# A two-layer decoder trunk on one core: stores, adds and row loads of the first layer's last head re-placed, and two small matmul groups of the second layer re-formed

## The chip, the cores and the metric

The kernel runs on one core of one Trainium2 chip. The metric is device microseconds of one execution; less is better. The core's engines are named as in the profile: PE (TensorE), DVE (VectorE), ACT (ScalarE), POOL (GpSimd), SP (SyncE); PEld is the loading of weights into PE.

## The reference, cut to what matters

Two residual layers over x of 512 tokens by 2048 channels, everything in fp32.

```python
for i in range(2):
    hn = rms_norm(x, norm_w[i])
    x = x + (diff_attention_mixer if i == 0 else rwkv7_mixer)(hn, ...)

# layer 0: 8 heads, two sets of scores each, 256 value channels per head
q, k, v, gate = split(h @ w_in)                      # w_in 2048 x 8192
q, k = rope(rms_norm(q)), rope(rms_norm(k))
a = softmax(q0 k0) - lam * softmax(q1 k1)            # causal
o = rms_norm(a @ v) * (1 - lambda_init) * silu(gate)
out = o @ w_out

# layer 1: RWKV-7, 32 heads of 64 channels
r, k, v, g, dw, da = split(mix(h @ w_in))            # mix: with the token before
kk = k * k_k
kk = kk / max(sqrt(sum over a head's channels of kk * kk), 1e-12)
for t in range(512):                                 # S: 64 x 64 per head
    S = S * w[t] + (S @ -kk[t]) (kk * a)[t]^T + v[t] k[t]^T
    y[t] = S @ r[t]
out = (group_norm(y) + bonus) * silu(g) @ w_out
```

## The kernel before, in words

Matrix products that need fp32 accuracy are made of three products of halves: each operand is a high part (wh, hH) and the rest (wl, hL), and `mm3` sums high x high, high x low, low x high. ACT casts wh from the loaded tile wraw (L105), DVE subtracts to get wl (L106). The 512-column matmuls named pp at L122 and L568 are most of PE's work.

**First layer.** The heads come one after the other. `unit_head` makes the projections of head h by products of blocks in halves of the matrix (a 2 x 2 scheme with fewer products), group by group: `all_groups` goes over N = 4 weight tiles, for each the split (L105, L106), then 12 matmuls at L568. Ta, Tb, Tc, Td (`g.Ts`, name `chained`) are four weight tiles of 512 KB that stay and are turned from one block's weights into the next by an accumulating DMA that POOL issues (`add_w`, L86), which adds another block of the matrix in memory to the tile. For the last head (h = 7, `last`) the order is: y, the block of T, S1, S2, `square`, `third`, S4. During S2 each of Ta to Td gets its next addend after its products, and four more tiles b0 to b3 (`b22`, named wraw) get theirs, for `third`. `s4` loads ("reloads") four more weight tiles on SP's queue into wraw.

While head h's matmuls run, the attention of head h - 1 is carried out in steps: a `Chain` counts matmuls (`tick`) and puts a step behind every so many of them. For one block of 128 tokens the steps are scores, softmax, turned weights (L364), weighted values o, norm, then `turn_y`: the 128 x 256 outputs y are transposed into PSUM (yt), ACT writes their high part yTh (L399), DVE the rest yTl (L401), and ACT issues the stores of both to the scratch tensors ys (L386). yTh has a place of its own, yTl one with the tag "th", one buffer each. Tile places are named by tags; S1's sums have the places sA and sA2, S2's sB, and so on. The reciprocal square roots on DVE (rs_i, rs_t, L64 to L71) belong to the norms.

After head 7 the kernel goes on to the output projection (`unit_tok` with da_w_out, L122). Its left operand are the rows of ys, loaded back by SP into tiles hH and hL (L931), 14 pairs of 256 KB tiles; the last two pairs are head 7's and stay on the chip.

**Second layer.** The heads are taken in 16 pairs. For each pair: projections (pp at L122), decays and keys (`stage1`), `stage2`, `gram` (gp at L1304: products of all chunks of 64 tokens), a forward substitution on DVE (`t_solve`, 31 steps, L1361 and L1363), `t_combine` (below), and a scan of eight chunks (sm at L1475, L1486, L1493; ACT copies rhs at L1478 and VS at L1488 between them), then the outputs Y (L1515, L1519). They are pipelined: gp of pair j + 1 comes right after the first part of `t_combine` of pair j.

`t_combine` completes the inverse of a 64 x 64 triangular matrix from two solved halves of 32 x 32: for each head and chunk a product px <- T, G (L1394), a copy to X (L1397), and a product px <- TT, X (L1404), copied to TT (L1407). Each is a matmul of 32 rows by 32 columns, placed by `tile_position` on a 32 x 32 tile of the array: the first product has head 0 on rows 0 and columns 32, head 1 on rows 64 and columns 96. There are 8 chunks x 2 heads = 16 matmuls at each line; in the trace a plain fp32 matmul is two records, so 32. Both heads write the same PSUM tile px.

The squares of the keys are summed for each head by two matmuls at L1210 and L1211 with a matrix of ones, after a split of the squares into sHx (ACT) and sLx (DVE); the 2 x 512 result is copied (ssl, L1291) and stored by SP for `t_solve`.

The order on each engine is set when the program is built: a scheduler takes instructions by priority (`high_priority`, the offsets SOLVE and SCAN) and by the explicit `issue_after`.

Of the kernel before, what the change touches and what calls it, by code (L numbers as in the profile page):

```python
# [326 lines left out]
def attention(g, h, qkT, qkL, sq, V, VL, G, gap, rows=None, keys=()):  # L327
# [56 lines left out]

    def store(i, ts, y):
        nc.scalar.dma_start(out=g.ys[i][h * 256 : (h + 1) * 256, ts].rearrange("(c p) t -> p c t", p=P),  # L386
                            in_=y[:].bitcast(F32))

    def turn_y(t):
        pt = g.ps.tile([P, 512], F32, name="yt", tag="pb")  # L390
        for i in range(2):
            nc.tensor.transpose(pt[:, i * P : (i + 1) * P], blocks[t].y[:, i * P : (i + 1) * P], g.ident[:])
        ts = slice(t * P, (t + 1) * P)
        pv = pt[:, :256].rearrange("p (c q) -> p c q", c=2)
        if rows is None:
            hi = w.tile([P, 2, P], F32R, name="yTh", tag="yTh", bufs=1)
            lo = w.tile([P, 2, P], F32R, name="yTl", tag="th", bufs=1)
            for c in range(2):
                nc.scalar.activation(hi[:, c], pv[:, c], AF.Copy, scale=g.subw[:, c : c + 1])  # L399
            for c in range(2):  # L400
                nc.vector.scalar_tensor_tensor(lo[:, c], pv[:, c], g.subw[:, c : c + 1], hi[:, c].bitcast(F32),  # L401
                                               ALU.mult, ALU.subtract)
            store(0, ts, hi)
            due.append((1, ts, lo))
            if h == NH - 2:
                store(*due.pop())
            return
        if t == 0:
            last.extend([[g.hp.tile([P, T], F32R, name=n, tag=n) for n in ("hH", "hL")] for _ in range(2)])
        for c, (hh, hl) in enumerate(last):  # L410
            nc.scalar.activation(hh[:, ts], pv[:, c], AF.Copy, scale=g.subw[:, c : c + 1])
            g.rowsplit = nc.vector.scalar_tensor_tensor(hl[:, ts], pv[:, c], g.subw[:, c : c + 1],
                                                        hh[:, ts].bitcast(F32), ALU.mult, ALU.subtract).ins
# [118 lines left out]
def unit_head(g, aps, h, t1s, sq, turned):  # L532


    nc = g.nc
    c1, c2 = qk_cols(aps, h), vg_cols(aps, h)
    acc1 = g.work.tile([P, 2, 512], F32, name="acc1", tag="acc1", bufs=1)
    acc = [None, None, acc1[:, 0], acc1[:, 1]]
    q = [t[:] for t in t1s]
    N = NH4 // KG  # L540
    last = h == NH - 1

    def pair():
        return [g.pp.tile([P, 512], F32, name="pp", tag="pp") for _ in range(2)]

    def load(i, k0, parts):
        pool, tag, bufs = (g.work, "Te", 1) if i == N - 1 else (g.wraw, "wraw", 3)
        raw = pool.tile([P, KG, 512], F32, name="wraw", tag=tag, bufs=bufs)
        load_w(g, raw, parts, k0 + i * KG, slice(0, KG))
        return raw  # L550

    def split(raw):
        return split_w(g, None, KG, 512, 0, raw)

    def block(k0, t0):
        return lambda k, t: [x[k0 + k][:, t0 + t * P : t0 + (t + 1) * P] for x in (g.hH, g.hL)]

    def form(nm, i):
        return lambda k, t: [x[:, t * P : (t + 1) * P] for x in g.sums[nm][i * KG + k]]

    def products(out, lhs, raw, start=False, end=False):
        wt = split(raw)
        for t in range(2):
            first = start
            for lo in range(2):
                for k in range(KG):
                    for x in lhs(k, t)[: 2 - lo]:
                        m = nc.tensor.matmul(out[t][:], x, wt[lo][:, k, :], start=first, stop=end and lo == 1 and k == KG - 1,  # L568
                                             skip_group_check=True)
                        tick(g, m)  # L570
                        first = False

    def all_groups(out, lhs, raw, start=False, end=False, then=None, also=None):
        added = None
        for i in range(N):
            r = raw(i)
            products(out, lhs(i), r, start and i == 0, end and i == N - 1)
            for x, k0 in [(r, then)] + ([(also[i], (c2, 0))] if also else []) if then else []:
                with g.tc.issue_after(added) if added else ExitStack():
                    added = add_w(g, x, k0[0], k0[1] + i * KG)  # L580

    def s4(out, keep, start=False, end=False):
        def raw(i):
            keep.append(load(i, NH4, c2))
            return keep[-1]
        all_groups(out, lambda i: form("S4", i), raw, start, end, None if last else (c2, 0))

    chained = lambda i: g.Ts[i]
    y = pair()
    all_groups(y, lambda i: block(NH4 + i * KG, 0), lambda i: load(i, NH4, c1), True, True)  # L590
    copy_out(g, q[:2], y)
    y = pair()
    all_groups(y, lambda i: block(i * KG, 0), chained, True, False, (c2, 0))
    take(g, q[:2], y)
    X = pair()
    all_groups(X, lambda i: form("S1", i), chained, True, last, (c2, NH4))
    copy_out(g, acc[2:], X)
    b22 = []
    if last:
        b22 += [load(i, NH4, c2) for i in range(N)]  # L600
    else:
        s4(X, b22, end=True)
        G, acc[:2] = gates(g)
        copy_out(g, acc[:2], X)
    all_groups(y, lambda i: form("S2", i), chained, then=(c1, NH4), also=last and b22)
    if last:
        G, acc[:2] = gates(g)
    take(g, acc[:2], y, ALU.subtract, acc[2:] if last else None)

    def square():  # L610
        X = pair()
        all_groups(X, lambda i: block(NH4 + i * KG, 256), chained, True, True)
        return X

    def third():
        for i in range(N):
            products(y, form("S3", i), b22[i], end=i == N - 1)
        take(g, acc[2:], y, ALU.subtract)

    head_qk(g, t1s, sq, [0, 1])  # L620
    if last:
        copy_out(g, q[2:], square())
        third()
        take(g, q[2:], y)
        head_qk(g, t1s, sq, [2, 3])
        turned()
        X = pair()
        s4(X, [], True, True)
        take(g, acc[:2], X)
        return head_vg(g, h, acc, G)  # L630
    turned()
    third()
    copy_out(g, q[2:], y)
    values = head_vg(g, h, acc, G)
    X = square()
    first_tiles(g, aps, h + 1)
    take(g, q[2:], X)
    head_qk(g, t1s, sq, [2, 3])
    return values
# [156 lines left out]
def layer0(g, aps):  # L796
# [3 lines left out]
    with ExitStack() as cx:  # L800
# [127 lines left out]
        for k in range(KT - 2):  # L928
            rows.append([g.hp.tile([P, T], F32R, name=n, tag=n) for n in ("hH", "hL")])
            for x, d in zip(rows[k], g.ys):  # L930
                loaded = nc.sync.dma_start(out=x[:].bitcast(F32), in_=d[k * P : (k + 1) * P, :]).ins  # L931
        ch = Chain(g, attention(g, h, *before, 20, rows, rest), 16)

        def all_rows(n, _):
# [279 lines left out]
def stage1(g, j, k, up):  # L1214
# [45 lines left out]

    def keys():
        nc.vector.tensor_mul(p.BK[:], p.BK[:], l[:, :, None, :].to_broadcast([P, NC_, 2, C]))
        k2 = w.tile([P, T], F32, name="k2", tag="thg", bufs=1)
        nc.scalar.activation(k2[:], k[:], AF.Square, scale=col("kk"))
        p.k2 = split_act(g, k2[:], w, "x")
        nc.vector.tensor_add(p.gam[:, 0 : NC_ - 1], m[:, 0 : NC_ - 1], m[:, 1:NC_])
        nc.scalar.activation(p.gam[:, 0 : NC_ - 1], p.gam[:, 0 : NC_ - 1], AF.Exp)

# [15 lines left out]
def gram(g, j, p, before):  # L1284

    nc, w, BK = g.nc, g.work, p.BK
    ps = g.ps.tile([P, 512], F32, name="pt", tag="pa", bufs=1)
    sum_channels(g, ps[:2, :], g.ones[:, 0 : P : C], p.k2)
    ss = w.tile([2, T], F32, name="ssl", tag="thg", bufs=1)
    with g.tc.high_priority(offset=SOLVE):  # L1290
        nc.scalar.copy(ss[:], ps[:2, :])  # L1291
        for half in range(2):
            nc.sync.dma_start(
                out=g.ltd[j % 2, half, :, :, HALF, :],
                in_=ss[:].rearrange("h (c b t) -> h c b t", c=NC_, b=2)[:, :, half, :])
    p.G = w.tile([P, NC_, 2, 2, C], F32, name="G1", tag="G1", bufs=2)
    p.BKT = w.tile([P, NC_, P], F32, name="BKT", tag="BKT", bufs=2)
    halves = []
# [73 lines left out]
def t_combine(g, j, p, lead):  # L1372
# [16 lines left out]
    yield GAP_T  # L1389
    N = NC_ * HALF  # L1390
    blocks = [(h, h * C, slice(h * C, h * C + HALF), slice(h * C + HALF, h * C + C)) for h in range(2)]
    for h, b0, lo, hi in blocks:
        for c in range(NC_):
            nc.tensor.matmul(px[hi, c * HALF : (c + 1) * HALF], p.G[lo, c, 0, h, HALF:C], T1[lo, c, :],  # L1394
                             start=True, stop=True, tile_position=(b0, b0 + HALF))
    for _, _, _, hi in blocks:
# [2 lines left out]
        r_ = slice(b0, b0 + C)  # L1399
        nc.scalar.copy(p.G[r_, :, 0, h, :], p.AR[r_, :, 0, :])  # L1400
    yield GAP_X
    for h, b0, lo, hi in blocks:
        for c in range(NC_):
            nc.tensor.matmul(px[lo, N + c * HALF : N + (c + 1) * HALF], X[hi, c, :], TT[hi, c, h, HALF:C],  # L1404
                             start=True, stop=True, tile_position=(b0 + HALF, b0))
    for h, b0, lo, _ in blocks:
# [365 lines left out]
```

## Time and profile before

| | |
|---|---|
| Time, three runs | 2114.43, 2110.9, 2113.84 us; median 2113.84 |
| Profiled execution | 2111.84 us, span 2110.1, mean granted clock 0.997 |
| PE busy | 2076.8 us, 98% of the span |
| DVE / ACT / POOL busy | 76% / 55% / 18% |
| First layer's stretch of this change | about 660 to 735 us of the span |
| Second layer's pairs | L1394 first at 1025.4, last at 1923.9 us |

A row of a timeline gives the start in us, the length in us, engine, line, operation, out<-in with shapes, the count of instructions drawn together, and in brackets the idle time of the engine before it with what ended that. A row of the windows gives the busy time and count of each engine, the granted clock of PE, the share of the DMA engines and GB/s. A row of DMA issues ends with the median us from issue to landing.

### The profile page before, as it was taken

What the parts mean: (1) busy time and instruction counts of PE and PEld (TensorE: products, weight loads), DVE (VectorE), ACT (ScalarE), POOL (GpSimd) and SP (SyncE); (2) the same over time, 40 slices, a digit from 0 to 9 for tenths busy, and PEclk for the clock granted to TensorE, in tenths of its full rate; (3) what the DMA queues carried; (4) which work ended last, traced back from release to release, by engine and by line L of the source; (5) the groups of instructions that cost most, each with busy time, mean ns of one, the idle gap of its engine ahead of it and who ended that gap; (6) DMA issues with size and microseconds to landing.
All of it is one profiled execution on the core that took longest, in us unless ns stands there. A gap on an engine that the chain in (4) does not pass through costs nothing.

```text
span 2110.1 us, 34038 instructions
## 1 busy us (share of the span) xinstructions
PE 2076.8 (98%) x11852; PEld 1690.5 (80%) x11852; DVE 1602.6 (76%) x4129; ACT 1153.6 (55%) x2278; POOL 370.4 (18%) x727
## 2 busy tenths in 40 slices
PE   9999999999999999999999999999999999999999
PEld 7888888888887788878777778888877787877887
DVE  6988888889887876576777778877777887767645
ACT  5765656566565544355465555565555556555322
POOL 1021111201112000101122221222222122221001
PEclk9999999999999999999999999999999999999999
DMA  8487877878778946623232332323333232345655
GB/s 268 153 173 190 181 170 187 166 188 177 173 183 176 307 149 179 150 88 96 90 87 89 90 90 84 94 83 92 99 95 86 85 94 86 97 138 180 190 159 121
DMA packets 159484, 294.60 MB, mean 140 GB/s; under 512 B 64352, under 2 KB 81760, under 8 KB 159312
## 3 DMA queue, kind: packets, MB, share of 16 engines
q1 hardware_dynamic: 110848, 184.91, 28.1%
q0 software_dynamic: 23808, 83.54, 21.5%
q10 hardware_dynamic: 24656, 23.97, 3.5%
q8 instruction: 93, 1.52, 0.3%
q14 instruction: 79, 0.65, 0.1%
HBM read 268.71 MB, written 23.66 MB: 139 GB/s over the span
## 4 chain that ended last, share of the span: by engine, by line
PE 74%; DVE 17%; issue 3%; ACT 3%; DMA 2%; ACTq 0%; DVEq 0%; SPq 0%
PE pp L122 33%; PE pp L568 22%; PE pt L122 4%; DVE wl L106 4%; DVE tmpl L1361 3%; DVE Tm L1363 2%; DVE VS L1497 2%; PE gp L1304 1%; ACT wh L105 1%; PE sc L122 1%; PE o L122 1%; PE sm L1475 1%; PE lora L122 1%; PE z L122 1%; PE sm L1486 1%
## 5 line engine op out<-in xcount | busy, mean ns | idle before, releaser
L106 DVE TENSOR_TENSOR wl<-wraw,wh 128x1024 fp32r<-128x1024 f32 (+2 forms) x291 | 357.7, 1229 | 211.0 <-ACT wh L105 202.2
L105 ACT CAST wh<-wraw 128x1024 fp32r<-128x1024 f32 (+2 forms) x291 | 303.6, 1043 | 266.1 <-PE pp L122 135.2
L122 PE MATMUL pp<-hL,wh 128*128 128x512 f32 x1024 | 414.7, 405 | 0.0
L122 PE MATMUL pp<-hH,wh 128*128 128x512 f32 x1024 | 413.8, 404 | 0.0
L122 PE MATMUL pp<-hH,wl 128*128 128x512 f32 x1024 | 413.6, 404 | 0.0
L122 PEld LDWEIGHTS pp<-hH,wh 128*128 128x128 f32 x1024 | 193.6, 189 | 34.3
L122 PEld LDWEIGHTS pp<-hL,wh 128*128 128x128 f32 x1024 | 193.5, 189 | 33.3
L122 PEld LDWEIGHTS pp<-hH,wl 128*128 128x128 f32 x1024 | 193.6, 189 | 32.4
L568 PE MATMUL pp<-wh,hH 128*128 128x512 f32 x448 | 176.8, 395 | 0.0
L568 PE MATMUL pp<-wh,hL 128*128 128x512 f32 x448 | 175.8, 392 | 0.0
L122 PE MATMUL pp<-wh,hH 128*128 128x512 f32 x372 | 145.6, 392 | 1.8 <-ACT hH L1092 1.8
L122 PE MATMUL pp<-wh,hL 128*128 128x512 f32 x372 | 146.4, 394 | 0.2
L122 PE MATMUL pp<-wl,hH 128*128 128x512 f32 x372 | 145.9, 392 | 0.5 <-DVE wl L106 0.5
L1481 POOL COPY SA<-VS 64x64 f32<-64x64 f32 x224 | 69.9, 312 | 425.0 <-DVE VS L1497 386.0
L1361 DVE SCALAR_TENSOR_TENSOR tmpl<-LT,Tm 128x60 f32<-128x60 f32 (+24 forms) x496 | 133.6, 269 | 11.4
L568 PE MATMUL pp<-wl,hH 128*128 128x512 f32 x448 | 140.4, 392 | 0.0
L1363 DVE TENSOR_TENSOR Tm<-Tm,tmpl 128x60 f32<-128x60 f32 (+24 forms) x496 | 104.4, 211 | 11.3
L1478 ACT COPY rhs<-sm 64x64 f32<-64x64 f32 x256 | 52.8, 206 | 89.3 <-PE sm L1475 85.9
L568 PEld LDWEIGHTS pp<-wl,hH 128*128 128x128 f32 x448 | 84.4, 188 | 17.3
L568 PEld LDWEIGHTS pp<-wh,hH 128*128 128x128 f32 x448 | 84.2, 188 | 17.3 <-issue 0.3
L568 PEld LDWEIGHTS pp<-wh,hL 128*128 128x128 f32 x448 | 84.2, 188 | 16.3
L1488 ACT COPY VS<-sm 64x64 f32<-64x64 f32 x256 | 52.7, 206 | 71.9 <-PE sm L1486 67.3
(397 smaller groups left out, 4417.6 us busy)
## 6 DMA issues: line engine op xcount, KB each, us to landing
wraw<-in_rw_w_in_dram SPq DMA_DIRECT2D x128, 512.0 KB
wraw<-in_da_w_in_dram SPq DMA_DIRECT2D x75, 512.0 KB
wraw<-in_da_w_in_dram POOLq DMA_DIRECT2D x28, 512.0 KB, 6.6
wraw<-in_da_w_out_dram SPq DMA_DIRECT2D x26, 512.0 KB
wraw<-in_rw_w_out_dram SPq DMA_DIRECT2D x26, 512.0 KB
Ta<-in_da_w_in_dram POOLq DMA_DIRECT2D x21, 512.0 KB, 5.5
Tb<-in_da_w_in_dram POOLq DMA_DIRECT2D x21, 512.0 KB, 5.5
Tc<-in_da_w_in_dram POOLq DMA_DIRECT2D x21, 512.0 KB, 5.5
```

What stands on the lines that cost most here:

```text
L105: a = nc.scalar.copy(hi[:, ks], raw[:, ks])
L106: d = nc.vector.tensor_sub(lo[:, ks], raw[:, ks], hi[:, ks].bitcast(F32))
L122: m = nc.tensor.matmul(out, a, b, start=s, stop=e, skip_group_check=skip)
L568: m = nc.tensor.matmul(out[t][:], x, wt[lo][:, k, :], start=first, stop=end and lo == 1 and k == KG - 1, skip_group_check=True)
L1304: m = nc.tensor.matmul(gp[h][:, i * P : (i + 1) * P], BK[r_, c0 + i, :, :], p.AR[r_, c0 + i, :, :], start=True, stop=True)
L1361: nc.vector.scalar_tensor_tensor(tt, LT[:, i : i + 1, i + 1 :].to_broadcast([P, s, n]), n2[:, i : i + 1], Tm[:, 0:s, i : i + 1].to_broadca ...
L1363: nc.vector.tensor_add(Tm[:, 0:s, i + 1 :], Tm[:, 0:s, i + 1 :], tt)
L1475: nc.tensor.matmul(sm[:, 0:P], both(p.G[:, c, 0]), both(VS[:, c]), start=True, stop=True)
L1478: nc.scalar.copy(rhs[r_, :], sm[r_, h * C : h * C + C])
L1481: nc.gpsimd.tensor_copy(p.SA[r_, c - 1, :], VS[r_, c, h, :])
L1488: g.copied = nc.scalar.copy(VS[r_, c, h, :], sm[r_, P : P + C])
L1497: g.state = nc.vector.scalar_tensor_tensor(VS[r_, c + 1, h, :], s_, p.gam[r_, c : c + 1], Sg[r_, :], ALU.mult, ALU.add)
```

## The change

Five edits.

1. In the attention of head 6 (`h == NH - 2`, which runs during head 7's projections) the turned outputs of all four token blocks go into one tile yT on the place sA2, each block in its own part, instead of yTh and yTl in turn.
2. In S2 of the last head the adds are issued in another order: b0 after Ta, and b1, b2, b3 after Td.
3. The loads of the rows of ys are issued behind the first reload of S4.
4. In `t_combine` both products go over chunks outside and heads inside, so that the two heads' matmuls take turns.
5. The keys' squares are kept in fp32 (no split) and summed by four matmuls of 128 tokens each, which write 32 rows apiece of one PSUM tile; the copy is 128 x 128, and the stores read it from there. k2 and ssl have places of their own.

```diff
     def store(i, ts, y):
...
-                            in_=y[:].bitcast(F32))
+                            in_=y.bitcast(F32))
...
-            hi = w.tile([P, 2, P], F32R, name="yTh", tag="yTh", bufs=1)
-            lo = w.tile([P, 2, P], F32R, name="yTl", tag="th", bufs=1)
+            if h == NH - 2:
+                if t == 0:
+                    last.append(w.tile([P, NT, 2, 2, P], F32R, name="yT", tag="sA2", bufs=1))
+                hi, lo = last[0][:, t, 0], last[0][:, t, 1]
+            else:
+                hi = w.tile([P, 2, P], F32R, name="yTh", tag="yTh", bufs=1)[:]
+                lo = w.tile([P, 2, P], F32R, name="yTl", tag="th", bufs=1)[:]
...
-            for x, k0 in [(r, then)] + ([(also[i], (c2, 0))] if also else []) if then else []:
+            adds = [(r, then, i)] if then else []
+            if also:
+                adds += [(also[n], (c2, 0), n) for n in ((0,), (), (), (1, 2, 3))[i]]
+            for x, k0, n in adds:
                 with g.tc.issue_after(added) if added else ExitStack():
-                    added = add_w(g, x, k0[0], k0[1] + i * KG)
+                    added = add_w(g, x, k0[0], k0[1] + n * KG)
...
             for x, d in zip(rows[k], g.ys):
-                loaded = nc.sync.dma_start(out=x[:].bitcast(F32), in_=d[k * P : (k + 1) * P, :]).ins
+                with tc.issue_after(g.reloaded):
+                    loaded = nc.sync.dma_start(out=x[:].bitcast(F32), in_=d[k * P : (k + 1) * P, :]).ins
...
-        k2 = w.tile([P, T], F32, name="k2", tag="thg", bufs=1)
-        nc.scalar.activation(k2[:], k[:], AF.Square, scale=col("kk"))
-        p.k2 = split_act(g, k2[:], w, "x")
+        p.k2 = w.tile([P, T], F32, name="k2", tag="k2", bufs=1)
+        nc.scalar.activation(p.k2[:], k[:], AF.Square, scale=col("kk"))
...
-    sum_channels(g, ps[:2, :], g.ones[:, 0 : P : C], p.k2)
-    ss = w.tile([2, T], F32, name="ssl", tag="thg", bufs=1)
+    for t in range(NT):
+        nc.tensor.matmul(ps[t * 32 : t * 32 + 32, :P], g.ones[:, C - 16 : C + 16].bitcast(F32),
+                         p.k2[:, t * P : (t + 1) * P], start=True, stop=True, tile_position=(0, t * 32))
+    ss = w.tile([P, P], F32, name="ssl", tag="ssl", bufs=1)
...
-    for h, b0, lo, hi in blocks:
-        for c in range(NC_):
+    for c in range(NC_):
+        for h, b0, lo, hi in blocks:
             nc.tensor.matmul(px[hi, c * HALF : (c + 1) * HALF], p.G[lo, c, 0, h, HALF:C], T1[lo, c, :],
                              start=True, stop=True, tile_position=(b0, b0 + HALF))
...
-    for h, b0, lo, hi in blocks:
-        for c in range(NC_):
+    for c in range(NC_):
+        for h, b0, lo, hi in blocks:
             nc.tensor.matmul(px[lo, N + c * HALF : N + (c + 1) * HALF], X[hi, c, :], TT[hi, c, h, HALF:C],
                              start=True, stop=True, tile_position=(b0 + HALF, b0))
```

On POOL, in S2 of the last head, the adds stood in this order before (the wraw are b0, b1, b2 and b3):

```order
L86 DMA Ta<-in_da_w_in_dram 128x1024
L86 DMA wraw<-in_da_w_in_dram 128x1024
L86 DMA Tb<-in_da_w_in_dram 128x1024
L86 DMA wraw<-in_da_w_in_dram 128x1024
L86 DMA Tc<-in_da_w_in_dram 128x1024
L86 DMA wraw<-in_da_w_in_dram 128x1024
L86 DMA Td<-in_da_w_in_dram 128x1024
L86 DMA wraw<-in_da_w_in_dram 128x1024
```

Now they stand so:

```order
L86 DMA Ta<-in_da_w_in_dram 128x1024
L86 DMA wraw<-in_da_w_in_dram 128x1024
L86 DMA Tb<-in_da_w_in_dram 128x1024
L86 DMA Tc<-in_da_w_in_dram 128x1024
L86 DMA Td<-in_da_w_in_dram 128x1024
L86 DMA wraw<-in_da_w_in_dram 128x1024 x3
```

Tc and Td moved ahead of b1, and Td ahead of b2 too. On SP, at the end of the first layer's last head, the row loads (L931) and the first reloads (wraw<-in_da_w_in) stood so before:

```order
L78 DMA T_8567<-in_da_w_out_dram 128x1024
L931 DMA hL<-ys_76 128x512
L931 DMA hH<-ys_75 128x512 x2
L931 DMA hL<-ys_76 128x512 x2
L931 DMA hH<-ys_75 128x512 x2
L931 DMA hL<-ys_76 128x512
L931 DMA hH<-ys_75 128x512
L931 DMA hL<-ys_76 128x512
L931 DMA hH<-ys_75 128x512
L78 DMA wraw<-in_da_w_in_dram 128x1024
```

and now:

```order
L78 DMA T_8560<-in_da_w_out_dram 128x1024
L78 DMA wraw<-in_da_w_in_dram 128x1024
L942 DMA hH<-ys_75 128x512
L942 DMA hL<-ys_76 128x512
L78 DMA wraw<-in_da_w_in_dram 128x1024
L942 DMA hH<-ys_75 128x512
```

The first reload moved ahead of all row loads. On ACT, at the place of `t_combine` and `gram` in one pair of the second layer, the rows were before:

```order
L1132 ACTIVATE mixr<-pp,omu 128x512
L1400 COPY G_14222<-AR 64x8x64
L1397 COPY X<-px 32x256
L1291 COPY ssl<-pt 2x512
L1397 COPY X<-px 32x256
L1400 COPY G_14222<-AR 64x8x64
L1101 COPY sHx<-mixr 128x512
L1311 COPY G_14911<-gp 128x8x64 x4
L1407 COPY TT_9520<-px 32x8x32 x2
L105 COPY wh<-wraw 128x1024
L1478 COPY rhs<-sm 64x64 x2
```

and are now:

```order
L1143 ACTIVATE mixr<-pp,omu 128x512
L1112 COPY sHx<-mixr 128x512
L1303 COPY ssl<-pt 128x128
L1409 COPY X<-px 32x256 x2
L1412 COPY G_14199<-AR 64x8x64 x2
L1323 COPY G_14886<-gp 128x8x64 x4
L1419 COPY TT_9513<-px 32x8x32 x2
L105 COPY wh<-wraw 128x1024
L1490 COPY rhs<-sm 64x64 x2
```

The cast of mixr moved ahead of the copies that follow the first px block, and ssl to the head of those copies.

More of the change, by code (lines that the diff above doesn't have):

```diff
@@ L548, in load @@
         raw = pool.tile([P, KG, 512], F32, name="wraw", tag=tag, bufs=bufs)
-        load_w(g, raw, parts, k0 + i * KG, slice(0, KG))
+        g.loaded = load_w(g, raw, parts, k0 + i * KG, slice(0, KG))
         return raw
@@ L584, in raw @@
             keep.append(load(i, NH4, c2))
+            if last and i == 0:
+                g.reloaded = g.loaded
             return keep[-1]
@@ L1287, in gram @@
     ps = g.ps.tile([P, 512], F32, name="pt", tag="pa", bufs=1)
-    sum_channels(g, ps[:2, :], g.ones[:, 0 : P : C], p.k2)
-    ss = w.tile([2, T], F32, name="ssl", tag="thg", bufs=1)
+    for t in range(NT):
+        nc.tensor.matmul(ps[t * 32 : t * 32 + 32, :P], g.ones[:, C - 16 : C + 16].bitcast(F32),
+                         p.k2[:, t * P : (t + 1) * P], start=True, stop=True, tile_position=(0, t * 32))
+    ss = w.tile([P, P], F32, name="ssl", tag="ssl", bufs=1)
     with g.tc.high_priority(offset=SOLVE):
-        nc.scalar.copy(ss[:], ps[:2, :])
-        for half in range(2):
+        nc.scalar.copy(ss[:], ps[:, :P])
+        for h in range(2):
             nc.sync.dma_start(
-                out=g.ltd[j % 2, half, :, :, HALF, :],
-                in_=ss[:].rearrange("h (c b t) -> h c b t", c=NC_, b=2)[:, :, half, :])
+                out=g.ltd[j % 2, :, h, :, HALF, :].rearrange("b (q c) t -> q c b t", q=NT),
+                in_=ss[16 * h : P : 32, :].rearrange("q (c b t) -> q c b t", c=2, b=2))
     p.G = w.tile([P, NC_, 2, 2, C], F32, name="G1", tag="G1", bufs=2)
```

## The prediction

> **What bounds the kernel now.** I read the page's busy times first, then the waits of PE, then timelines at the places that the change touches.
>
> ```profile
> PE 2076.8 (98%) x11852; PEld 1690.5 (80%) x11852; DVE 1602.6 (76%) x4129; ACT 1153.6 (55%) x2278; POOL 370.4 (18%) x727
> ```
>
> ```profile
> PE sm L1475 <- DVE VS L1497: 9.7, 28, 0.8
> PE pt L364 <- DVE rs_i L65: 5.8, 1, 5.8
> ...
> PE sm L1486 <- ACT rhs L1478: 1.5, 4, 0.4
> ```
>
> PE is busy for 98% of the span. So a change pays only where it takes matmul time off PE, or takes away one of the few waits in the second view (columns: total us, times, longest). The largest single one is 5.8 us, once, in the first layer. The profiled execution took 2111.84 us with a span of 2110.1; the median of the runs shown is 2113.84, which is 2.0 above it. I sum against the profiled execution and add the 2.0 at the end. What a measurement of this kernel can tell from no change is about 0.2%, 4.2 us.
>
> **Part 1: places of their own for head 6's outputs.** The timeline around that wait:
>
> ```profile
> 680.43 1.10 PE L568 MATMUL pp<-wh,sB 128*128 128x512 f32 x4
> ...
> 681.93 0.62 ACT L399 ACTIVATE yTh<-yt,subw 128x128 fp32r<-128x128 f32 x2 [2.36 <-DMA ys<-yTh]
> ...
> 687.08 0.35 DVE L401 SCALAR_TENSOR_TENSOR yTl<-yt,subw,yTh 128x128 fp32r<-128x128 f32 x1 [7.07 <-DMA ys<-yTl]
> ...
> 687.80 1.11 PE L364 MATMUL pt<-ident,a 128*128 128x128 f32 x4 [5.81 <-DVE rs_i L65]
> ```
>
> ```profile
> 688.57 2.05 PE L568 MATMUL pp<-wh,sB 128*128 128x512 f32 x4
> ...
> 691.27 1.54 PE L568 MATMUL pp<-wh,sB 128*128 128x512 f32 x4
> ```
>
> DVE stands 7.07 us at yTl (L401), because the one buffer of yTl is still being read by the store of the token block before. Behind it in DVE's queue are the rows of the next block's rs_i, and the transposes of PE come after those: that is the 5.81 us. After the change all four blocks have their own 2 KB in a tile on S1's second place, so neither ACT's 2.36 nor DVE's 7.07 us is left. After the idle time PE also runs slower:
>
> ```profile
> 681.00:693.00 12.00, 6.19 (x21) 4.75 (x20) 5.09 (x19) 2.31 (x5) 1.02 (x2) 0.72 1.06 213
> ```
>
> The granted clock (before the last two columns) is 0.72 in this stretch. Four matmuls at 680.43 take 1.10 us, at 688.57 they take 2.05 and at 691.27 still 1.54: 0.95 and 0.44 too much, and I put about 0.8 on the two wl matmuls between them and on the transposes. So the stall is worth 5.8 + 0.95 + 0.44 + 0.8 = 8.0 us. The new tile can be written only after S1's last matmuls have read that place; those stand a few matmuls ahead of the first turned block, so I take 0, at most 0.5 us on ACT.
>
> **Part 2: the order of the adds.** Without the stall PE comes to the next blocks 8 us earlier. The adds that make them are slow, since the DMA engines are full in that stretch (share 1.06 in the row above):
>
> ```profile
> Td<-in_da_w_in_dram POOLq DMA_DIRECT2D x1, 512.0 KB, 12.4
> ```
>
> ```profile
> 680.30 0.84 POOL L86 DMA_DIRECT2D Td<-in_da_w_in_dram  x1 [0.29 <-DVE so L378]
> ```
>
> ```profile
> 700.00 1.05 ACT L105 CAST wh<-Td 128x1024 fp32r<-128x1024 f32 x1 [0.70 <-PE pp L568]
> ```
>
> Td is issued at 680.30, lands 12.4 us later (the last number of the first row) at 692.7, and is cast at 700.00. With 8 us off, that cast comes at 692.0: in the old order it would be late by 0.7 us. In the old order Tb, b1, Tc and b2 stand before it on the queue, so the 12.4 us are up to five transfers of some 2.5 us. In the new order b1 and b2 go behind it: it lands 5 us sooner, at 687.7, 4.3 us ahead of its cast. The adds of b1 and b2 that move back are read only after all of Td's products: 0 us, at most one transfer, 2.5.
>
> **Part 3: rows behind the reload.**
>
> ```profile
> 696.80 0.33 SPq L931 DMA_DIRECT2D hL<-ys  x1
> ...
> 705.21 0.33 SPq L78 DMA_DIRECT2D wraw<-in_da_w_in_dram  x1
> ```
>
> ```profile
> 729.02 0.39 PE L122 MATMUL pp<-wh,hH 128*128 128x512 f32 x1
> ```
>
> Eleven row loads stand ahead of the first reload on SP's queue now; afterwards all 28 stand behind it. The reload waits for its buffer, which follows PE, so it moves to about 705.2 - 8 = 697.2, and the rows start then instead of at 696.8. Their first reader moves to 721, 24 us later. 0 us; if this cover were gone it would be the 8 us that the rows have not moved forward.
>
> **Part 4: second layer, two heads in turn for T, and the sums.** Each of the 16 pairs of heads has these rows (one pair):
>
> ```profile
> 1434.35 1.09 PE L1394 MATMUL px<-T,G 32*32 32x32 f32 x32
> 1435.38 0.40 PE L1210 MATMUL pt<-sHx,ones 128*2 128x512 f32 x1
> 1435.61 0.40 PE L1211 MATMUL pt<-sLx,ones 128*2 128x512 f32 x1
> 1435.94 2.06 PE L1304 MATMUL gp<-AR,BK 64*128 64x128 f32 x32
> ...
> 1442.60 0.43 PE L1486 MATMUL sm<-rhs,TT 128*128 128x64 f32 x2
> ```
>
> The px block is 32 records, 16 of one head and then 16 of the other, in 1.09 us. Do two heads overlap? Two answers of the same timeline for windows of 0.14 us, the first inside head 0, the second where head 1 begins:
>
> ```profile
> 1434.35 0.53 PE L1394 MATMUL px<-T,G 32*32 32x32 f32 x11
> ```
>
> ```profile
> 1434.56 0.50 PE L1394 MATMUL px<-T,G 32*32 32x32 f32 x14
> ```
>
> In 0.53 us 11 records run (0.03 us from one to the next, once the length of one, 0.19, is off); at the border 14 fit in 0.50: the heads do run side by side there, in the same bank. If they do so throughout, a block needs 15 steps of 0.032 and one length, 0.5 + 0.19 = 0.69 instead of 1.09, so 0.40 less. There are two such blocks for each pair (L1394, L1404): 0.80 us of PE.
>
> The sums go from two matmuls that hold PE from 1435.38 to 1435.94, 0.56 us, to four of 32 columns by 128 in plain fp32, eight records. Price per record from another row:
>
> ```profile
> 1486.52 1.20 PE L1515 MATMUL Y<-VS,G 128*64 128x64 f32 x32
> ```
>
> Here 64 moving columns in two column tiles take (1.20 - 0.2) / 31 = 0.032 us a record, as long as 32 columns on one tile above, so two column tiles run side by side. 128 columns on one tile are then 0.13: eight cost 1.0 us in a row, 0.25 four abreast. I take 0.29, nearer the row with two abreast carried on: 0.27 less. PE saves 0.80 + 0.27 = 1.07 us per pair, at most; with the sums in a row 0.36.
>
> How much of it arrives is decided by ACT, which between this block and L1486 has no gap:
>
> ```profile
> 1435.08 0.62 ACT L1400 COPY G<-AR 64x512 f32<-64x512 f32 x1 [3.15 <-PE px L1394]
> 1435.72 0.36 ACT L1397 COPY X<-px 32x256 f32<-32x256 f32 x1
> 1436.11 0.57 ACT L1291 COPY ssl<-pt 2x512 f32<-2x512 f32 x1
> ...
> 1437.73 0.62 ACT L1101 CAST sHx<-mixr 128x512 fp32r<-128x512 f32 x1
> ...
> 1442.13 0.42 ACT L1478 COPY rhs<-sm 64x64 f32<-64x64 f32 x2
> ```
>
> ```profile
> 1434.07 0.75 DVE L1280 SCALAR_TENSOR_TENSOR mixr<-mixr,prm_hrk,f 128x512 f32<-128x512 f32 x1
> ```
>
> It works from 1435.08 to the end of rhs at 1442.55, and PE starts L1486 at 1442.60, with it. In the new order the cast of mixr stands first; its input is done at 1434.82, so it fits before the chain (-0.65 with its gap), and ssl of 128 columns costs about 0.25 instead of 0.57 (-0.32; X of 256 columns costs 0.36). But ssl now leads the chain and waits for the sums, which end some 0.63 + 0.57 us after the px block's start: the chain starts at +1.2 instead of +0.73 (+0.47). Sum: -0.50 us per pair. PE would be 1.07 early and waits the other 0.57 for rhs at L1486. DVE loses one subtraction of 512 columns per pair, beside a PE that doesn't wait for it: 0. So 16 x 0.50 = 8.0 us; bounds 0 and 16 x 1.07 = 17.1 us.
>
> The Trainium skill, TensorEngine Tiling (Array Packing), Restrictions and Gotchas, says that different row tiles cannot access the same PSUM bank at the same time. Both heads of px write one bank, so by it turns would give nothing or cost; the border row above speaks against it.
>
> **The sum.** 2111.84 - 8.0 (part 1) - 0 - 0 - 8.0 (part 4) = 2095.8, and 2.0 more against the median: **2097.8 us**, faster by 0.8%.
>
> **The rivals.**
> - *All of PE's saving arrives.* If ACT is relieved more than I sum (X's copies or rhs not bound as I think), 16 x 1.07 = 17.1 us come instead of 8: 2113.84 - 25.1 = 2088.7. For: ACT is busy 55% only. Against: the unbroken chain above.
> - *Turns give nothing.* The px blocks stay at 1.09, so ssl comes 0.40 later and -0.50 becomes -0.10 per pair: 2113.84 - 8.0 - 1.6 = 2104.2. Against: the border row.
> - *The four sums run in a row.* They take 1.0 us, ssl comes 0.75 later, and -0.50 becomes +0.25 per pair: 2113.84 - 8.0 + 4.0 = 2109.8. Against: the row of L1515. The Trainium skill, TensorE: Matmul & The Clock Gate, The mechanism, says that weight loads overlap matmuls in flight only when the row group differs; the four sums share all rows and differ in columns, so it speaks for this rival.
> - *The stall moves.* The store wait goes, and PE then waits for the adds or reloads, as DMA has 8 us less for the same bytes at a share of 1.06. Only the second layer's 8.0 is left: 2105.8. Against: the 4.3 us of slack of Td in the new order.
> - *Slower: tiles of one bank exclude each other.* If each change of head waits until the record before has left, a block's 32 records cost 0.19 each, 6.1 us instead of 1.09: 5 us x 32 blocks = 160 us, about 2266. It turns the total to slower from (8.0 + 4.2) / 1024 records = 0.012 us more per record. Against: 14 records in 0.50 us at the border.
>
> **How the numbers follow.** My forecast 0.56; all of it arrives 0.12; turns give nothing 0.09; the sums in a row 0.08; the stall moves 0.08; tiles exclude each other 0.04; several small losses that eat everything 0.03. The range runs from just under the first rival, 2087, to 2109, which takes in the two at 2104 and 2106 with some 3 us for runs and for a stall worth less, and leaves out about 0.15 at the top. My own case alone: 2094 to 2101. A gain of over 4.2 us holds in the first three cases and nearly all of the stall's, with some of the sums': 0.87; within 0.2%: 0.08; slower: 0.05.
>
> **What would show it.** Right: the 5.8 us row of L364 is gone and the clock is whole from 681 to 693; px blocks of about 0.7 us; PE from the px block to gp about 0.9 us instead of 1.6; a new wait of PE for rhs at L1486, 0.5 us in each pair. Wrong: px blocks still at 1.09; eight records of the sums spread over 1 us; a wait of ACT's cast of Tb to Td for a DMA; no wait at L1486 and twice the gain.

## The result and the profile after

The changed kernel takes 2092.88 us (median of 4 runs, 2091.67 to 2093.54) against 2114.14 (2110.9 to 2116.03): ratio 0.990, 95% interval 0.989 to 0.9914, so 18 to 23 us less. The forecast was 2097.8 in a range of 2087 to 2109.

PE's busy time and its waits, from the page and the waits of the changed kernel:

```profile
PE 2057.0 (98%) x11948; PEld 1674.9 (80%) x11948; DVE 1591.5 (76%) x4113; ACT 1139.9 (54%) x2262; POOL 372.8 (18%) x727
```

```profile
PE sm L1487 <- DVE VS L1509: 10.0, 29, 0.9
PE sm L1498 <- ACT rhs L1490: 6.0, 14, 0.8
...
PE o L122 <- DVE y L383: 1.1, 1, 1.1
```

The 5.8 us wait of L364 is gone, and PE's busy time, in which matmuls at a lower clock count longer, is 20 us shorter. The wait of sm for ACT's rhs grew from 1.5 us in 4 places to 6.0 in 14: that is the new wait of the second layer. One for DVE's y in the first layer is new too.

The two traces hold the same matmuls of 512 columns in the same order, so the start of each can be subtracted from that of its counterpart. The difference in each stretch (times of before):

| Stretch, us | After minus before, us |
|---|---|
| start to 680 | +0.1 (+0.6 at 60, given back by 680) |
| 680 to 760, first layer's last head | -6.4 |
| 760 to 1020 | -0.1 |
| 1020 to 1050, first pair of the second layer | -2.9 |
| 1050 to 1290, next four pairs | -3.7 |
| 1290 to 1900, ten pairs | -5.4 |
| 1900 to the end | -0.1 |

The sum is that of the two spans, 2110.1 and 2091.7. The medians differ by 21.3 us: the profiled execution of before (2111.84) lay 2.3 below its median, that of after (2093.39) 0.5 above.

First layer, timeline of the changed kernel at the place of the old stall, and its windows:

```profile
681.88 0.60 PE L364 MATMUL pt<-ident,a 128*128 128x128 f32 x4
...
683.72 1.09 PE L573 MATMUL pp<-wh,sB 128*128 128x512 f32 x4
...
686.83 0.35 PE L122 MATMUL o<-V,at 128*128 128x256 f32 x1 [1.08 <-DVE y L383]
```

```profile
681.00:693.00 12.00, 10.92 (x57) 8.98 (x56) 9.74 (x33) 5.46 (x10) 2.82 (x4) 1.00 1.05 211
```

The transposes follow the matmuls without a gap, four matmuls take 1.09 us, and the granted clock is 1.00 in this stretch, though the DMA engines are as full as before (1.05).

Second layer, PE and ACT in one pair of the changed kernel:

```profile
1420.50 0.69 PE L1406 MATMUL px<-T,G 32*32 32x32 f32 x32
1421.13 0.43 PE L1299 MATMUL pt<-k,ones 128*32 128x128 f32 x8
1421.48 2.06 PE L1316 MATMUL gp<-AR,BK 64*128 64x128 f32 x32
1423.47 0.69 PE L1416 MATMUL px<-TT,X 32*32 32x32 f32 x32
...
1428.19 0.43 PE L1498 MATMUL sm<-rhs,TT 128*128 128x64 f32 x2 [0.36 <-ACT rhs L1490]
```

```profile
1421.02 0.62 ACT L1112 CAST sHx<-mixr 128x512 fp32r<-128x512 f32 x1 [2.95 <-DVE mixr L1290]
1421.62 0.27 ACT L1303 COPY ssl<-pt 128x128 f32<-128x128 f32 x1
1421.91 0.74 ACT L1409 COPY X<-px 32x256 f32<-32x256 f32 x2
1422.67 1.26 ACT L1412 COPY G<-AR 64x512 f32<-64x512 f32 x2
...
1427.71 0.43 ACT L1490 COPY rhs<-sm 64x64 f32<-64x64 f32 x2
```

The px block is 0.69 us long instead of 1.09, the sums cost 0.35 to the next start instead of 0.56, and from the start of one px block to the other it is 2.97 us instead of 3.57. ACT works from 1421.02, when DVE has written mixr, to 1428.14 without a gap worth naming; PE waits for its last step.

### The profile page after: what moved, and what is told of

Same layout as the page of the kernel before. It is cut to its first block, busy times and chain, and to the rows that moved or that the text cites. A ratio compares the mean times of both kernels' runs of the same rounds, so it can differ in the third digit from the quotient of the medians.

```text
span 2091.7 us, 34159 instructions
## 1 busy us (share of the span) xinstructions
PE 2057.0 (98%) x11948; PEld 1674.9 (80%) x11948; DVE 1591.5 (76%) x4113; ACT 1139.9 (54%) x2262; POOL 372.8 (18%) x727
## 4 chain that ended last, share of the span: by engine, by line
PE 71%; DVE 19%; ACT 5%; issue 4%; DMA 1%; ACTq 0%; SPq 0%; DVEq 0%
PE pp L122 31%; PE pp L573 22%; PE pt L122 5%; DVE wl L106 4%; DVE tmpl L1373 4%; DVE Tm L1375 3%; ACT wh L105 2%; DVE VS L1509 2%; PE gp L1316 1%; PE sc L122 1%; PE o L122 1%; PE sm L1487 1%; PE lora L122 1%; PE z L122 1%; PE sm L1498 1%
```

## The experiments

Each ratio is to the kernel before, whose median lay between 2112.49 and 2113.34 us in these sets. "Period" is the distance from one pair's first px block to the next pair's in the steady pairs, the ten between 1290 and 1900 us, read from the traces (their median): 61.40 us before, 60.85 after.

**Places alone.** Only `yT`'s hunk and the store's slice are put into the kernel before.

```diff
+            if h == NH - 2:
+                if t == 0:
+                    last.append(w.tile([P, NT, 2, 2, P], F32R, name="yT", tag="sA2", bufs=1))
+                hi, lo = last[0][:, t, 0], last[0][:, t, 1]
...
```

> Only the own places for head 6's outputs; adds, rows and the second layer as before. My theory: the store wait is the whole stall, and the clock's return with it, so the 5.8 us wait of L364 is gone; about 1.2 us come back as a wait for DVE's y (L383) as in the changed kernel; Td's cast comes at about 693 and its add lands at 692.7, so the old order of adds costs 0 to 0.7 us: first layer -6 to -7 us, and nothing in the second layer. Rival (the stall moves): without the new order and the rows behind the reload, PE waits for Tc, Td or the reloads, and less than 3 us are left.

Measured: 2107.0 us, ratio 0.9971 (0.9959 to 0.9982). In the trace the first layer's stretch gives 8.0 us up to 700 us of before, and 2.4 come back by 720. ACT and PE there:

```profile
697.64 0.62 ACT L404 ACTIVATE yT<-yt,subw 128x128 fp32r<-128x128 f32 x2 [1.01 <-PE yt L392]
700.36 0.37 ACTq L386 DMA_DIRECT2D ys<-yT  x1
700.85 1.05 ACT L105 CAST wh<-wraw 128x1024 fp32r<-128x1024 f32 x1 [2.11 <-DMA hL<-ys]
```

```profile
706.26 0.50 PE L573 MATMUL pp<-wh,hH 128*128 128x512 f32 x1 [0.94 <-ACT wh L105]
```

yT is ready at 698.26, but ACT issues its store at 700.36, and the cast behind it names a row load (hL<-ys) as releaser of 2.11 us of idle time. So the store wait was the whole first stall, as the theory had it, and what comes back is neither the adds nor DVE's y: it is ACT, held by the issue of a store. The trace also names what holds it. A completion semaphore is the counter by which a transfer tells that it is done. ACT's and SP's DMAs are given the same eight of them in turn, and an issue first waits until the transfer that had its semaphore before is done. This store is given semaphore 109, which the row load issued at 692.50 has; that load's end comes at 700.29, and the wait ends at 700.31. In the changed kernel the same store is given 107, last used by a store of ACT at 671.34, and it goes out 0.03 us after yT is ready.

**The old order of adds**, else the changed kernel:

```diff
-                adds += [(also[n], (c2, 0), n) for n in ((0,), (), (), (1, 2, 3))[i]]
...
+            for x, k0 in [(r, then)] + ([(also[i], (c2, 0))] if also else []) if then else []:
...
```

> The changed kernel with the adds in the old order. My theory: Td would land at about 692.7 and is cast at 693.3 in the changed kernel, so 0 to 0.7 us slower than the changed kernel. Rival: Tc and Td come late by one transfer each, 2.5 us or more slower, with ACT waiting for a DMA at its casts L105.

Measured: 2093.26 us (2091.82 to 2093.7), the changed kernel's time. The DMA issues and ACT's casts of this run:

```profile
Td<-in_da_w_in_dram POOLq DMA_DIRECT2D x1, 512.0 KB, 12.1
```

```profile
694.29 1.05 ACT L105 CAST wh<-Td 128x1024 fp32r<-128x1024 f32 x1 [0.47 <-PE pp L573]
```

Td's add, issued at 682.15, lands at 694.21, and its cast starts at 694.29. The row names PE, but the cast waits for the add's semaphore too, which came within 0.01 us of PE's. It starts 2.14 us after the cast of Tc, against 1.58 in the changed kernel, so the old order does make it about half a us late, as the theory had it; PE's matmuls behind it go on without a break. The new order (Td in 8.9 us in the changed kernel) buys slack and no time.

**Rows free of the reload**, else the changed kernel:

```diff
-                with tc.issue_after(g.reloaded):
-                    loaded = ...
+                loaded = ...
```

> The changed kernel with the rows no longer behind the reload. In the run with the places alone, a store of ACT (ys<-yT) was issued 2.1 us late, behind a row load by the releaser, and the cast behind it let PE wait. Theory now: the same here, ACT's store and cast about 2 us late at 700 us, PE loses 2 to 3 us: about +2.5 against the changed kernel, 2095.5. Rival (my prediction's reading, that this edit is worth nothing): the time of the changed kernel within 1 us.

Measured: 2094.06 us, 2091.14 to 2100.63. ACT and PE around 703 us of this run:

```profile
703.27 0.37 ACTq L386 DMA_DIRECT2D ys<-yT  x1
703.75 1.05 ACT L105 CAST wh<-wraw 128x1024 fp32r<-128x1024 f32 x1 [2.68 <-DMA hL<-ys]
```

```profile
704.85 0.50 PE L573 MATMUL pp<-wh,hH 128*128 128x512 f32 x1 [0.53 <-ACT wh L105]
```

The mechanism came back, ACT's store and cast 2.7 us late, again by semaphore 109 of a row load, but PE lost only 0.53 us here in one wait, 1.6 in all until 720. In the four traces with the rows behind the reload (this change, the old adds, and two below) no store waits for a row load, so that the edit takes ACT's wait away is shown. Its worth is not: the median difference of 1.2 us lies inside the spread of these runs, and the first layer's stretch gains 6.5 us here against 6.4 in the changed kernel. The six runs spread over 9.5 us, but in the profiled one, the slowest (2100.63), the time over the changed kernel lies elsewhere: 3.0 us before 680 and 4.9 after 1900.

**Both edits of the second layer alone** (edits 4 and 5 of the change in the kernel before):

> Both second-layer edits (heads in turn, unsplit sums), none of the first layer's. On ACT the scheduler here keeps sHx<-mixr between the copies (G<-AR, ssl, X, G<-AR, sHx, G<-gp) instead of ahead of ssl. My theory (ACT's chain decides): the same matmul saving, 1.0 us per pair on PE up to the end of the second px block, but the chain starts at +0.75 and loses only 0.32, so rhs comes 0.3 us earlier instead of 0.56: about -0.3 in each of the 12 steady pairs and the same 5.5 us in the first four: -9 us. Rival (PE alone decides): -12 us as in the changed kernel.

Measured: 2101.37 us, ratio 0.9942 (0.9925 to 0.9959). The premise about ACT's order was wrong: in the trace sHx stands ahead of ssl, as in the changed kernel, and the period is 60.80. From 720 to 1900 this kernel gains 12.5 us, the changed one 12.1, both with 1.6 us of a lower clock in the profile of before (see below). So the second layer's part belongs to these two edits, and the order of ACT was not tested by this run. The first layer's lost time was shared out differently in this execution, with the same code as before:

```profile
PE pp L568 <- ACT wh L105: 3.2, 1, 3.2
PE pt L364 <- DVE rs_i L65: 1.7, 1, 1.7
PE o L122 <- DVE y L383: 0.6, 1, 0.6
```

It came to 0.4 us less than in the profile of before: a shorter stall at L364 was paid back by a later one. The same holds for the other four runs below with the old first layer: L364 waits 1.9 to 3.2 us in them, and the whole stretch takes from 1.5 us less to 0.2 us more than in the profile of before.

**Heads in turn alone:**

```diff
-    for h, b0, lo, hi in blocks:
-        for c in range(NC_):
+    for c in range(NC_):
+        for h, b0, lo, hi in blocks:
...
```

> Only the heads in turn for T, with the split sums, first layer as before. PE's blocks fall by 0.4 each, 0.8 per pair. Theory (ACT's chain decides): the chain G<-AR, ssl 2x512, X, G<-AR, sHx, G<-gp, TT, wh, rhs is as long as before and starts with the end of the px block, so rhs stays at 8.2 after the block's start and the steady pairs give 0 to -0.1 each; only the first three pairs, where no gram stands behind the block, give 3 to 4 us: -3 to -5 in the second layer. Rival (PE decides): -0.8 a pair, -13.

Measured: 2106.9 us, ratio 0.9972 (0.9961 to 0.9982). PE in a steady pair:

```profile
1431.71 0.69 PE L1394 MATMUL px<-T,G 32*32 32x32 f32 x32
...
1439.95 0.43 PE L1486 MATMUL sm<-rhs,TT 128*128 128x64 f32 x2 [0.71 <-ACT rhs L1478]
```

Both px blocks are 0.40 shorter, and the period is 61.39 against 61.40: all of it is lost at L1486, which comes 8.24 us after the block's start, as before (8.25). The waits of PE for rhs add up to 10.2 us in 14 places here. Only the first pairs and the last gain: 5.5 us up to 1900 us of before, 3.6 of them up to 1160 and 2.8 in the last stretch, less 0.9 between. (Of the 3.6, 1.6 are a lower clock in the profile of before, see below.) So ACT's chain, not PE, ends this stretch.

**Unsplit sums alone** (edit 5 only):

> Only the unsplit sums, px blocks head after head, first layer as before. PE saves 0.2 us per pair, ACT's chain loses 0.3 (ssl of 128 columns) but G<-AR, ssl wait for their inputs as before, and sHx stays in the chain: theory -0.1 to -0.3 per pair, -1.6 to -5 in the second layer. With the turns alone it would then not add up to the -12 of both together: the two edits need each other, since with both the scheduler puts sHx ahead of the chain. Rival: each edit gives its own part, about -4 here.

Measured: 2107.78 us, ratio 0.9981 (0.9971 to 0.9991); the period is 61.24, so -0.16 per steady pair. With the turns' 0.01 that makes 0.17; both together give 0.55. The two edits don't add up: with the turns alone ACT is the limit, with the sums alone PE is.

**The sums in a row**, else the changed kernel:

```diff
-        nc.tensor.matmul(ps[t * 32 : t * 32 + 32, :P], ..., tile_position=(0, t * 32))
+        nc.tensor.matmul(ps[:32, t * P : t * P + P], ..., tile_position=(0, 0))
...
```

> The changed kernel with the four sums on one column tile (written to four stretches of 128 columns of 32 rows) instead of four tiles side by side; ssl is then 32x512, and ACT copies X before ssl. It prices the column tiles: theory eight records at about 0.12 us, 1.0 us instead of 0.35 from the first record to gp; the px block to the second px block grows by 0.65; on ACT ssl comes 0.3 us later and costs 0.3 more, so rhs is about 0.3 later per steady pair: +3 to +5 us against the changed kernel. Rival (the four were serial anyway): px to gp unchanged at 0.98 us.

Measured: 2098.13 us, ratio 0.9937 (0.9925 to 0.9949), 5.3 us more than the changed kernel.

```profile
1488.75 1.06 PE L1299 MATMUL pt<-k,ones 128*32 128x128 f32 x8
1489.74 2.06 PE L1316 MATMUL gp<-AR,BK 64*128 64x128 f32 x32
```

The same eight records take 0.99 us to the next start instead of 0.35, 0.12 each: on four column tiles they do run side by side. The 5.3 us are not the price of the tiles alone, since ssl of 512 columns also takes ACT 0.57 us instead of 0.27; the period is 61.06, 0.21 more than in the changed kernel.

**The copies of AR on DVE**, else the changed kernel; and the same edit on the kernel before, and on the one with turns alone:

```diff
-        nc.scalar.copy(p.G[r_, :, 0, h, :], p.AR[r_, :, 0, :])
+        nc.vector.tensor_copy(p.G[r_, :, 0, h, :], p.AR[r_, :, 0, :])
```

> The changed kernel with the two copies G<-AR (1.26 us per pair on ACT) done by DVE, which has about 2 us of idle time at this place. My theory: the new wait of PE for rhs at sm<-rhs, 0.36 us with the rest of the break about 0.45, is ACT's chain and goes away: -0.45 in about 13 pairs, -6 us against the changed kernel, 2087. Rival: another wait ends there (sm<-VS for DVE, or X late), no gain.

> The kernel before, with only the two copies G<-AR of each pair moved from ACT to DVE. My theory: in the kernel before ACT's chain and PE end about together at the first sm<-rhs of a pair, with some 0.1 to 0.2 us of PE's time lost there, so relieving ACT alone gives 0.1 to 0.2 us in each steady pair (period 61.2 to 61.3 instead of 61.4), -2 to -3 in the second layer, though it takes as much off ACT as in the run that gave 0.64 per pair on top of the change. Rival: ACT bounded these pairs all along, -0.6 per pair or more.

> Heads in turn for T alone, which gave a steady period of 61.40 (nothing), and the two copies G<-AR on DVE. My theory: the turns take 0.8 us off PE per pair, which was lost in the wait for ACT's rhs; with ACT relieved it arrives: period about 61.4 - 0.8 - 0.15 = 60.45. Rival: PE's saving is lost elsewhere too (DVE's VS, the split of the squares): 61.0 or more.

| Kernel | ACT copies AR: period, us | DVE copies AR: period, us | time with DVE's copies, us (ratio) |
|---|---|---|---|
| before | 61.40 | 61.21 | 2110.35 (0.9988, 0.9976 to 1.0) |
| turns alone | 61.39 | 60.42 | 2095.57 (0.9921, 0.9907 to 0.9936) |
| changed | 60.85 | 60.21 | 2082.31 (0.9854, 0.9833 to 0.9874) |

PE and ACT of the changed kernel with DVE's copies:

```profile
1418.52 0.69 PE L1416 MATMUL px<-TT,X 32*32 32x32 f32 x32
...
1422.73 0.33 PE L1498 MATMUL sm<-rhs,TT 128*128 128x64 f32 x2
```

```profile
1421.74 0.43 ACT L1490 COPY rhs<-sm 64x64 f32<-64x64 f32 x2
```

rhs ends at 1422.17, half a us ahead of PE, and the wait is gone; 1.26 us off ACT are worth 0.64 per pair here, 0.97 with the turns alone and only 0.19 in the kernel before, where PE came as late as ACT. The time of that last run can't be told from no change (its interval reaches 1.0); its period can. The changed kernel with DVE's copies is the fastest of all that ran, by 10.6 us against the changed kernel where 6 were expected.

## Why the prediction was right, step by step

- **The stall (part 1), -8.0.** Right in mechanism and in size: by the matmuls' starts 8.0 us are gained up to 692 us in the changed kernel. What the sum left out is what is late next when a stall goes: 1.3 us come back at once with PE's wait for DVE's y (1.08), and 0.3 after it, so -6.4 stayed. The same first layer gave -6.4 again in the run with the sums in a row and -7.7 in the run with DVE's copies, where that wait is absent; what decides whether it appears stays open. The 5.8 us at L364 are those of one execution: five others waited 1.7 to 3.2 us there and lost most of the rest later.
- **The adds (part 2), 0.** Right. Td landed 8.9 us after its issue, not in the 7.4 that the sum put, and still 4.1 us ahead of its cast. In the old order the cast is late by 0.5 us, near the 0.7 of the prediction, and costs PE nothing.
- **The rows (part 3), 0.** The sum was right in that the edit itself adds no wait, but its reading missed what the edit is for. I considered only the readers of the rows, with 24 us of slack; the two runs with the rows free show that SP's row loads hold a store that ACT has to issue, 2.1 and 2.7 us, through a completion semaphore that both use in turn, and a cast of weights stands behind it. I asked what the moved loads meet on SP, and not what they hold on ACT. With neither the rows nor the adds moved, part 1 kept 5.6 of its 8.0 us.
- **The px blocks, 0.69 us.** Measured 0.69. The border row of the trace before was enough to tell it. The Trainium skill, TensorEngine Tiling (Array Packing), Restrictions and Gotchas, says that different row tiles cannot access one PSUM bank at the same time. Here head 0 on rows 0 and head 1 on rows 64 write the one tile px, one bank by the prediction, in 0.69 us for both, as long as one head alone takes by its 15 steps of 0.032 and one length of 0.19 (0.67). The measurement decides against the rule for this form.
- **The sums, 0.29.** Measured 0.35, 0.06 more than put; PE saves 0.60 to the second px block where I had 0.67, and 1.00 in all where I had 1.07. The Trainium skill, TensorE: Matmul & The Clock Gate, The mechanism, lets weight loads overlap matmuls in flight only when the row group differs. The trace doesn't agree: the four sums share all rows, a weight load and a matmul of each of the four start within 0.03 us, and the eight records take 0.35 side by side against 0.99 in a row.
- **ACT's chain, -0.50 per pair.** Measured -0.55 in the period, with the wait at L1498 that was forecast (PE could start 1.00 earlier, L1498 comes 0.56 earlier, and 0.36 of the difference is the wait shown). The rival "all of PE's saving arrives" fell for the reason given; with DVE's copies it came true (1.19 per pair).
- **16 equal pairs.** This is where 8.0 became 12. The first five pairs gave 6.6 instead of 2.5. No gram stands behind the px block of the first three, so ACT's chain is shorter there, and PE's saving arrives; that this is the reason is argued, not tested by a run of its own. In the first pair the clock matters as well. PE idled 1.15 us ahead of px before, now 0.57, and seven matmuls behind it took 0.63 us each before (granted clock 0.59 from 1026 to 1030 us). Before and after:

```profile
1025.42 1.09 PE L1394 MATMUL px<-T,G 32*32 32x32 f32 x32 [1.15 <-DVE y L1418]
1026.44 0.55 PE L122 MATMUL pp<-hH,wh 128*128 128x512 f32 x1
1026.79 0.63 PE L122 MATMUL pp<-hL,wh 128*128 128x512 f32 x1
```

```profile
1018.42 0.69 PE L1406 MATMUL px<-T,G 32*32 32x32 f32 x32 [0.57 <-DVE y L1430]
1019.04 0.50 PE L122 MATMUL pp<-hH,wh 128*128 128x512 f32 x1
1019.38 0.39 PE L122 MATMUL pp<-hL,wh 128*128 128x512 f32 x1
```

Now they take 0.39 to 0.40. The clock makes up 1.6 of the first pair's 2.9 us, and that is luck: of the six traces with 1.15 to 1.77 us of idle time at this place, two show the lower clock and four don't. So the forecast of 16.0 us came near 18.4 of the profiled pair of runs with two errors that partly cancel: 1.6 too much in the first layer, 4 too little in the second. Between the forecast 2097.8 and the measured 2092.88 lie 4.9 us: 2.4 are these, and 2.5 are the 2.0 us that were added for the distance of a profiled execution from the median, which came out at -0.5 in the changed kernel.

## What to carry to other kernels

When two engines end a stretch almost together, price an edit on both: 0.8 us off PE gave 0.01, 1.26 us off ACT gave 0.19, and the two edits together 0.97 per pair. After removing a wait, ask of every instruction that can block its engine's queue, DMA issues among them, and not only of the readers of the data; of a DMA issue, ask also which transfer had its completion semaphore before. And read the pairs at the start and the end of a pipeline by themselves; they have other neighbours than the steady ones.

## What the runs showed of the hardware

- Two 32 x 32 tiles on different rows and columns, writing different partitions of one PSUM tile, run at full pace side by side: 32 records in 0.69 us instead of 1.09.
- Four tiles of 128 rows and 32 columns run side by side too: eight records of 128 moving columns in 0.35 us instead of 0.99.
- ACT stood for 2.1 and 2.7 us at issuing a store whose data was ready. What it waited for is the completion semaphore that a row load of SP had and that the store was to use next, so this is a wait of the program and not shown to be one of the DMA queues.
- After 5.8 us of idle time the granted clock was 0.57 over the next 5.2 us. After short idle times the length alone does not tell: ahead of the first pair's px, 1.15 and 1.25 us (before, and before with DVE's copies) were followed by a clock of 0.67 and 0.66 over 4 us, and 1.18, 1.25, 1.30 and 1.77 us in four other runs by 1.00; near 1916 us, 0.82 us idle in the run with the sums alone were followed by 0.63, and 1.98 us in the one with the places alone by 1.00.
